# Low parts of the mixers' weights by an adding transfer instead of a subtraction on GpSimd or VectorE, with small steps moved off VectorE

## The chip, the cores and the metric

The kernel runs on one core of one Trainium2 chip. The metric is the device time of one execution in microseconds (us), median of three runs.

## The reference

One decoder layer over 512 tokens of width 1024, batch 1. `u = rmsnorm(x)` is projected by one wide matrix `w_in` into the inputs of two mixers. The first is a gated delta rule with 8 heads of 128 (q, k, v, an output gate z, a decay and a beta per head); the second is a sparse attention with 8 query heads and 2 key heads, for which an indexer scores keys and keeps the best 128 per query. Both results are gated and added, multiplied by `w_out`, and added to x. Then comes a ConvGLU feed-forward of width 2816, and a last RMS norm.

```
u     = rmsnorm(x, g1);  proj = u @ w_in
qkv   = silu(causal_dwconv(proj[:, 0:3072], w, width 4));  q, k = l2norm(q), l2norm(k)
o_gdn = rmsnorm(delta_rule(q, k, v, decay, beta)) * silu(z)
score[t,s] = sum_h iw[t,h] * relu(iq[t,h] . layernorm(ik)[s]);  keep the top 128 causal s
o_dsa = softmax(q k^T on the kept keys) v
h     = x + (sigmoid(ga) * o_gdn + sigmoid(gb) * o_dsa) @ w_out
out   = rmsnorm(h + (silu(conv(up_gate)) * conv(up_val)) @ w_down)
```

All arithmetic is float32 at the interface.

## The kernel before, in words

Every large product is made of three TensorE passes in the rounded type float32r. Both operands are split into a high part (`hi`, the value rounded to float32r) and a low part (`lo`, what is left over), and a product is `hi*lo + lo*hi + hi*hi`. The function `passes` (L202, L203, L204) issues the three matmuls. The weights lie in DRAM as pieces of 128 x 1024 floats (512 KB). `load` issues one piece's transfer on SyncE's queue into a buffer `raw`; `piece` then lets ScalarE copy `raw` to `whi` (L194, which rounds) and another engine, GpSimd or VectorE, subtract `raw - whi` into `wlo` (L195). There are three buffers of each. A chunk is two pieces. `channel_major` multiplies a chunk with all 512 tokens into two PSUM banks of 128 channels each (24 matmuls of 512 columns per piece); `token_major` makes tokens the rows (48 matmuls of 256 columns per piece). PSUM has three banks named `acc` for these.

In program order: the start loads the transposed x (`xT`), splits it (`xgh`, `xgl`) and computes the attention's values (`dv`) and a small projection (`sp`: indexer key, decay, beta, indexer weights) while pieces arrive. The factors 1/rms of the four token blocks (`r4`) are turned into a row by four diagonal matrices `dg` and a matmul with ones (`rp`), giving `rB`. Then `uTh`, `uTl` (the split normalized input) are made, and the indexer queries `iq` come from two chunks on the un-normalized `xg`, scaled afterwards by `rB` (`iqf`). `gdn_half(0)` and `gdn_half(1)` each do six chunks (k, q, v of four heads), a causal convolution with SiLU on VectorE and ScalarE (`conv_silu`), transposes with sums of squares (`sumsq`), a triangular inverse by forward substitution (`nn`, `wi`, `tw`: 60 dependent VectorE steps between two round trips through DRAM, `bl`), and a recurrence over four chunks (`TR`, `upd`, `kS`, `o`). VectorE also finds the top 128 scores (`top`, `mask`). The attention's 32 items (`lg`, `pe`, `pT`, `oB`) and the twelve gate chunks (z, ga, gb, `token_major`) follow. After them `w_out` (8 pieces) and the feed-forward (44 and 22 pieces) run with the same `piece`, with VectorE (for the first two chunks of the feed-forward GpSimd) as the engine of the low part. The mixers have 62 pieces that go through `piece`; the three pieces of the start are split by `split` (L231 to L234).

The order within each engine's queue is not the program's: the framework's scheduler lays the instructions out by a simulated timeline and then fixes one static order per engine. Every engine runs its queue in order, so an instruction that waits holds all behind it on its engine.

Of the kernel before, what the change touches and what calls it, by code (L numbers as in the profile page):

```python
# [86 lines left out]
def hybrid_block(ctx: ExitStack, tc: tile.TileContext, x: bass.AP, xc: bass.AP, wp: bass.AP,  # L87
# [90 lines left out]


    pipe = ctx.enter_context(tc.tile_pool(name="pipe", bufs=1))  # L180
    pipe.tile([128, 16], F, name="pad1")
    pos = [0]

    def load():
        raw = pipe.tile([128, 1024], F, name="raw", bufs=3)
        nc.sync.dma_start(raw, wp[pos[0]])
        pos[0] += 1
        hi = pipe.tile([128, 1024], R, name="whi", bufs=3)
        lo = pipe.tile([128, 1024], R, name="wlo", bufs=3)
        return raw, hi, lo  # L190

    def piece(lo_engine):
        raw, hi, lo = load()
        A.copy(hi, raw)  # L194
        lo_engine.tensor_sub(lo, raw, hi.bitcast(F))  # L195
        return hi, lo

    def passes(o, lhs, rhs, first, last, shared=False):
# [29 lines left out]
        for tb in tbs:  # L228
            nc.sync.dma_start(xt[tb], x[128 * tb:128 * tb + 128])

    def split(raw, hi, lo):  # L231
        for eng, c in ((V, slice(0, 512)), (P, slice(512, 1024))):
            A.copy(hi[:, c], raw[:, c])
            eng.tensor_sub(lo[:, c], raw[:, c], hi[:, c].bitcast(F))  # L234

    load_xT(0)
    nc.sync.dma_start(ch, chan)
    dvp = [load()]
    load_xT(1, 2, 3)
    dvp.append(load())  # L240
    load_xT(4, 5, 6, 7)
    sp = load()
    load_x(0, 1, 2, 3)
# [16 lines left out]

    for k in range(KT):
        x_part(k)
        if k % 4 == 0:
            split(*dvp[k // 4])
        dv_mm(k)
    split(*sp)
    for k in range(KT):
# [6 lines left out]
    rp = tp("rp")  # L274
    for tb in range(NT):
        dg = sl.tile([128, 128], F, name="dg", bufs=2)
        V.tensor_scalar(dg, ident, r4[:, tb:tb + 1], None, op0=OP.mult)
        T.matmul(rp[:, 128 * tb:128 * tb + 128], ones, dg, start=True, stop=True)
    V.tensor_copy(rB, rp)
    sr.release()  # L280
# [11 lines left out]
    def token_major(eng):  # L292

        pcs = [piece(eng), piece(eng)]
# [9 lines left out]
    def channel_major(eng, src=None, second=P):  # L304
        pcs = [piece(eng), piece(second)]
# [54 lines left out]
    A.copy(ikh, ikp)  # L360
    V.tensor_sub(ikl, ikp, ikh.bitcast(F))
    iw = const.tile([128, NT, 8], F, name="iw")
    V.tensor_scalar(iw, sm[:, :, 80:88], float((H ** -0.5) * (IDXD ** -0.5)), None, op0=OP.mult)


    def sc8(name):
# [48 lines left out]
    for k in range(KT):  # L415
# [2 lines left out]
        A.copy(uTh[:, k], uv)  # L418
        (V, P)[k % 2].tensor_sub(uTl[:, k], uv, uTh[:, k].bitcast(F))

    iq = []
    for j in range(2):
        for t, p in enumerate(channel_major(P, xg)):
            iqf = PR.tile([128, 512], F, name="iqf", tag="t", bufs=5)
            V.tensor_mul(iqf, p, rB)  # L425
            for s in range(2):
                q = PR.tile([128, 512], R, name="iq", tag="dqo", bufs=9)
                src = iqf[64 * s:64 * s + 64]
                A.copy(q[0:64], src)
                V.tensor_sub(q[64:128], src, q[0:64].bitcast(F))  # L430
                iq.append(q)
# [37 lines left out]
    def gdn_half(hh):  # L469
# [14 lines left out]
        def sumsq(src, dst, keep):  # L484
            for c in range(NT):
                p = rec("kqt")
                for h in range(HH):
                    T.transpose(p[:, 128 * h:128 * h + 128], src[:, h, 128 * c:128 * c + 128], ident)
                for h in range(HH):
                    A.activation(sqj, p[:, 128 * h:128 * h + 128], AF.Square, accum_out=dst[:, 0, c, h:h + 1])  # L490
                if keep is not None:
                    V.tensor_copy(keep[:, c], p.rearrange("p (h d) -> p h d", d=128))


        for j in range(2):
            for t, p in enumerate(channel_major(P, second=V if hh else P)):
# [4 lines left out]
        ks = sc("ks", 5)  # L501
        rk, mk, nk, bk, kd = (ks[:, i] for i in range(5))
# [4 lines left out]
        V.tensor_mul(kd, rk, kde[:, :, hs])  # L507

        for j in range(2):
            for t, p in enumerate(channel_major(P, second=V if hh else P)):  # L510
# [8 lines left out]
        for c in range(NT):  # L519
            ge = PL.tile([128, 2, HH, 128], F, name="ge", tag="g4", bufs=2)  # L520
            r0 = c * H + HH * hh
            A.dma_start(ge[:, 0], bass.AP(tensor=gdr.tensor, offset=gdr.offset + r0 * 128,
                                          ap=[[0, 128], [128, HH], [1, 128]]))
            P.affine_select(out=ge[:, 1], in_=ge[:, 0], pattern=[[0, HH], [1, 128]], base=0,
                            channel_multiplier=-1, compare_op=OP.is_ge, fill=NEG)
            for h in range(HH):
                A.activation(ge[:, 1, h], ge[:, 1, h], AF.Exp, bias=nG[:, c, HH * hh + h:HH * hh + h + 1])
            A.activation(ge[:, 0], ge[:, 0], AF.Exp)
            cs = slice(128 * c, 128 * c + 128)
            for h2 in range(2):  # L530
# [12 lines left out]
            for h in range(HH):  # L543
                A.activation(kt[:, c, h], kt[:, c, h], AF.Identity, scale=kd[:, c, h:h + 1])


        for j in range(2):
            for t, p in enumerate(channel_major(P, second=V if hh else P)):
# [79 lines left out]
        for c in range(NT):  # L628
# [62 lines left out]


    dk = PR.tile([128, 2, 512], F, name="dk", tag="k4", bufs=2)
    for t, p in enumerate(channel_major(P)):
        A.copy(dk[:, t], p)
    dq = []
    for j in range(4):
        for t, p in enumerate(channel_major(P)):
            q = half_kb("dq")
            A.copy(q, p)  # L700
            dq.append(q)
# [64 lines left out]
        V.scalar_tensor_tensor(o, t, 1.0, o, op0=OP.add, op1=OP.mult)  # L766

    def z_chunk(j):
        for t2, p in enumerate(token_major(P)):
# [5 lines left out]

    def ga_chunk(j):
        bias = gate_bias(256 * j)
        for t2, p in enumerate(token_major(P)):
            gated(oAv[j][:, 2 * t2:2 * t2 + 2], p, bias)

    def gb_chunk(j):
        bias = gate_bias(1024 + 256 * j)
        for t2, p in enumerate(token_major(P)):
            tb = slice(2 * t2, 2 * t2 + 2)
            t = tmp("tg")
            V.tensor_add(t, p, bias)
# [252 lines left out]
```

## Time and profile before

| | us |
|---|---|
| median of 3 runs | 965.05 (963.51 to 967.03) |
| the profiled execution's own time | 965.41 |
| its span in the trace | 963.4 |
| TensorE busy | 923.5 (96%) |
| VectorE, ScalarE, GpSimd busy | 615.2, 439.7, 205.3 |

The span is the time from the first to the last instruction of the program. Matmuls are pipelined and their ends are modelled, so a busy TensorE is one that has matmuls in flight. The granted clock of TensorE in a stretch is a share of its full speed: 1.00 is 2.4 GHz and 0.50 is 1.2 GHz.

### The profile page before, as it was taken

The page shows a single profiled execution, that of the slowest core. Times are in us where ns is not written, and L with a number is a line of the kernel's source. Part 1 is how long each engine was busy: PE and PEld are TensorE (multiplying, and loading weights), DVE is VectorE, ACT ScalarE, POOL GpSimd, SP SyncE. Part 2 cuts the span into 40 slices and gives each one's busy share as a digit, 9 for nine tenths or more (in the row PEclk, how much of TensorE's full clock was granted, in tenths as well). Part 3 has the DMA queues.
Part 4 walks back from the last instruction along what each step waited for, and adds up shares of the span by engine and source line. Part 5 has one row for each costly group of instructions (what it writes and reads, how often), then busy time and mean ns, then how long its engine had stood idle before and what let it go on. Part 6 is the DMA issues. An engine that isn't in the chain of part 4 may idle for free.

```text
span 963.4 us, 14652 instructions
## 1 busy us (share of the span) xinstructions
PE 923.5 (96%) x5671; PEld 806.4 (84%) x5671; DVE 615.2 (64%) x1262; ACT 439.7 (46%) x938; POOL 205.3 (21%) x120
## 2 busy tenths in 40 slices
PE   8889998989999898899999999999999999999997
PEld 8768887767787797899999999888888888888886
DVE  5997999897638948755543637556655666522424
ACT  7436673422458653345544436444444444421313
POOL 2744343520211254211154022100000000000201
PEclk9999999998999999999999999999999999999999
DMA  8222222324310122311322223323232332323212
GB/s 322 93 87 88 88 72 83 100 65 110 111 45 25 64 77 85 98 55 50 137 72 91 85 90 97 100 87 102 96 104 94 88 110 87 110 90 107 88 66 87
DMA packets 39541, 89.29 MB, mean 93 GB/s; under 512 B 15632, under 2 KB 16944, under 8 KB 39472
## 3 DMA queue, kind: packets, MB, share of 16 engines
q1 hardware_dynamic: 24048, 82.05, 26.0%
q10 hardware_dynamic: 15424, 6.31, 2.7%
q8 instruction: 44, 0.72, 0.3%
q14 instruction: 25, 0.20, 0.1%
HBM read 85.18 MB, written 3.16 MB: 92 GB/s over the span
## 4 chain that ended last, share of the span: by engine, by line
PE 66%; DVE 22%; DMA 5%; ACT 3%; issue 2%; POOL 1%; ACTq 0%; SPq 0%; DVEq 0%; POOLq 0%
PE acc L202 17%; PE acc L204 17%; PE acc L203 17%; PE d L202 3%; PE d L203 3%; PE d L204 3%; DVE y L460 3%; DVE wi L585 2%; DVE mask L689 2%; DVE tw L583 2%; DVE top L688 2%; PE lg L728 1%; PE lg L710 1%; DMA ge<-gdr 1%; DMA nn<-bl 1%
## 5 line engine op out<-in xcount | busy, mean ns | idle before, releaser
L194 ACT CAST whi<-raw 128x1024 fp32r<-128x1024 f32 x136 | 142.3, 1047 | 175.7 <-PE acc L204 77.0
L195 POOL TENSOR_TENSOR wlo<-raw,whi 128x1024 fp32r<-128x1024 f32 x60 | 147.5, 2460 | 295.4 <-ACT whi L194 248.2
L195 DVE TENSOR_TENSOR wlo<-raw,whi 128x1024 fp32r<-128x1024 f32 x76 | 94.3, 1241 | 147.5 <-ACT whi L194 147.4
L203 PE MATMUL acc<-hTh,wlo 128*128 128x512 f32 (+1 forms) x368 | 139.8, 380 | 0.0
L202 PE MATMUL acc<-hTl,whi 128*128 128x512 f32 (+1 forms) x368 | 139.1, 381 | 0.2 <-DVE hTl L837 0.2
L204 PE MATMUL acc<-hTh,whi 128*128 128x512 f32 (+1 forms) x368 | 138.8, 380 | 0.0
L202 PE MATMUL acc<-uTl,whi 128*128 128x512 f32 x272 | 109.1, 402 | 5.3 <-DVE iqf L425 4.3
L203 PE MATMUL acc<-uTh,wlo 128*128 128x512 f32 x272 | 108.9, 400 | 5.1 <-DVE wlo L195 5.1
L204 PE MATMUL acc<-whi,uTh 128*128 128x256 f32 x384 | 113.3, 295 | 0.0
L202 PE MATMUL acc<-wlo,uTh 128*128 128x256 f32 x384 | 112.2, 292 | 0.0
L203 PE MATMUL acc<-whi,uTl 128*128 128x256 f32 x384 | 112.1, 292 | 0.0
L204 PE MATMUL acc<-uTh,whi 128*128 128x512 f32 x272 | 108.9, 400 | 0.0
L979 POOL TENSOR_TENSOR h<-h,gf 128x512 f32<-128x512 f32 (+1 forms) x8 | 10.6, 1344 | 338.6 <-ACT sq L975 338.6
L896 DVE SCALAR_TENSOR_TENSOR fy<-acc,ch,fy 128x511 f32<-128x511 f32 x88 | 65.8, 748 | 26.2 <-ACT fy L894 24.7
L202 PEld LDWEIGHTS acc<-hTl,whi 128*128 128x128 f32 x368 | 69.2, 188 | 13.5 <-DVE hTl L837 0.4
L204 PEld LDWEIGHTS acc<-hTh,whi 128*128 128x128 f32 x368 | 69.2, 188 | 13.1
L203 PEld LDWEIGHTS acc<-hTh,wlo 128*128 128x128 f32 x368 | 69.2, 188 | 13.1
L202 PEld LDWEIGHTS acc<-wlo,uTh 128*128 128x128 f32 x384 | 73.9, 193 | 1.6 <-issue 1.0
L204 PEld LDWEIGHTS acc<-whi,uTh 128*128 128x128 f32 x384 | 73.8, 192 | 1.7 <-issue 1.0
L203 PEld LDWEIGHTS acc<-whi,uTl 128*128 128x128 f32 x384 | 74.0, 193 | 1.2 <-issue 1.0
L202 PEld LDWEIGHTS acc<-uTl,whi 128*128 128x128 f32 x272 | 52.1, 192 | 16.6 <-DVE iqf L425 4.8
L203 PEld LDWEIGHTS acc<-uTh,wlo 128*128 128x128 f32 x272 | 52.1, 191 | 15.5 <-DVE wlo L195 5.5
(313 smaller groups left out, 1916.9 us busy)
## 6 DMA issues: line engine op xcount, KB each, us to landing
raw<-in_wp_dram SPq DMA_DIRECT2D x139, 512.0 KB, 3.4
xT<-in_xc_dram SPq DMA_DIRECT2D x8, 256.0 KB, 6.0
xt<-in_x_dram SPq DMA_DIRECT2D x4, 512.0 KB, 7.8
ge<-gdr ACTq DMA_DIRECT2D x8, 256.0 KB, 3.4
h<-in_x_dram SPq DMA_DIRECT2D x4, 512.0 KB, 6.0
out_dram<-h SPq DMA_DIRECT2D x8, 256.0 KB, 2.2
gbias<-in_rows_dram ACTq DMA_DIRECT2D x8, 128.0 KB, 3.1
nn<-bl ACTq DMA_DIRECT2D x4, 256.0 KB, 4.8
```

What stands on the lines that cost most here:

```text
L194: A.copy(hi, raw)
L195: lo_engine.tensor_sub(lo, raw, hi.bitcast(F))
L202: a = T.matmul(o, lh, rl, start=first, stop=False, skip_group_check=shared)
L203: T.matmul(o, ll, rh, start=False, stop=False, skip_group_check=shared)
L204: return a, T.matmul(o, lh, rh, start=False, stop=last, skip_group_check=shared)
L460: V.scalar_tensor_tensor(y[:, s:], p[:, :512 - s], cw[:, ti, 3 - s:4 - s], y[:, s:], op0=OP.mult, op1=OP.add)
L583: V.tensor_mul(w, wi[:, 0:c, j:j + 1].to_broadcast([128, c, m]), nn[:, j:j + 1, j + 1:].to_broadcast([128, c, m]))
L585: V.tensor_sub(wi[:, 0:c, j + 1:], wi[:, 0:c, j + 1:], w)
L688: V.max(top, score[b])
L689: V.match_replace(score[b], top, score[b], TAKEN)
L896: V.scalar_tensor_tensor(y[:, s:], p[:, :512 - s], fw[:, ti, 2 - s:3 - s], y[:, s:], op0=OP.mult, op1=OP.add)
L979: P.tensor_mul(hv, hv, gf[:, 512 * half + c.start:512 * half + c.stop])
```

## The change

The low part of a mixer's piece is no longer a subtraction. ScalarE writes `-raw`, rounded to float32r, into `wlo`; this is `-hi`. Then a transfer issued by GpSimd reads the same piece from DRAM once more and adds it to `wlo` in SBUF, which leaves `raw - hi`. `whi` is copied by ScalarE as before. So each of the 62 pieces has a second ScalarE pass and a second transfer of 512 KB, and no subtraction. `raw` has two buffers instead of three for the whole kernel, `wlo` four instead of three. `w_out` and the feed-forward keep the subtraction.

Small steps go with it. The indexer's 1/rms is left out of the queries and multiplied into the indexer's weights `iw`. The key's l2 factor `rk` is left out of `at` and `kt` and put into the scale of `vt` (`mk` for `bk`), so `at` of two heads is one product. The copy of the transposed keys (`keep`) and the diagonals `dg` go from VectorE to ScalarE. The pieces of the start are loaded in halves, split in quarters by ScalarE and VectorE alone, and the constants `ch` are loaded on ScalarE's queue.

```diff
-    def load():
-        raw = pipe.tile([128, 1024], F, name="raw", bufs=3)
-        nc.sync.dma_start(raw, wp[pos[0]])
+    def load(parts=1):
+        raw = pipe.tile([128, 1024], F, name="raw", bufs=2)
+        n = 1024 // parts
+        for k in range(parts):
+            nc.sync.dma_start(raw[:, n * k:n * k + n], wp[pos[0]][:, n * k:n * k + n])
         pos[0] += 1
         hi = pipe.tile([128, 1024], R, name="whi", bufs=3)
-        lo = pipe.tile([128, 1024], R, name="wlo", bufs=3)
+        lo = pipe.tile([128, 1024], R, name="wlo", bufs=4)
         return raw, hi, lo

-    def piece(lo_engine):
+    def piece(lo_engine=None):
+        w = wp[pos[0]]
         raw, hi, lo = load()
-        A.copy(hi, raw)
-        lo_engine.tensor_sub(lo, raw, hi.bitcast(F))
+        if lo_engine is None:
+            A.activation(lo, raw, AF.Copy, scale=-1.0)
+            P.dma_start(lo, w, accum_op=OP.add)
+            A.copy(hi, raw)
+        else:
+            A.copy(hi, raw)
+            lo_engine.tensor_sub(lo, raw, hi.bitcast(F))
         return hi, lo
...
-    def split(raw, hi, lo):
-        for eng, c in ((V, slice(0, 512)), (P, slice(512, 1024))):
+    def split(raw, hi, lo, n=512, ks=None):
+        for k in range(1024 // n) if ks is None else ks:
+            c = slice(n * k, n * k + n)
             A.copy(hi[:, c], raw[:, c])
-            eng.tensor_sub(lo[:, c], raw[:, c], hi[:, c].bitcast(F))
+            V.tensor_sub(lo[:, c], raw[:, c], hi[:, c].bitcast(F))
+
+    A.dma_start(ch, chan)
     load_xT(0)
-    nc.sync.dma_start(ch, chan)
-    dvp = [load()]
+    dvp = [load(2)]
     load_xT(1, 2, 3)
-    dvp.append(load())
+    dvp.append(load(2))
...
-        if k % 4 == 0:
-            split(*dvp[k // 4])
+        split(*dvp[k // 4], n=256, ks=[k % 4])
...
-        V.tensor_scalar(dg, ident, r4[:, tb:tb + 1], None, op0=OP.mult)
+        A.activation(dg, ident, AF.Identity, scale=r4[:, tb:tb + 1])
...
-    V.tensor_scalar(iw, sm[:, :, 80:88], float((H ** -0.5) * (IDXD ** -0.5)), None, op0=OP.mult)
+    V.scalar_tensor_tensor(iw, sm[:, :, 80:88], float((H ** -0.5) * (IDXD ** -0.5)),
+                           r4.unsqueeze(2).to_broadcast([128, NT, 8]), op0=OP.mult, op1=OP.mult)
...
-            iqf = PR.tile([128, 512], F, name="iqf", tag="t", bufs=5)
-            V.tensor_mul(iqf, p, rB)
...
-                src = iqf[64 * s:64 * s + 64]
+                src = p[64 * s:64 * s + 64]
...
-                    V.tensor_copy(keep[:, c], p.rearrange("p (h d) -> p h d", d=128))
+                    A.copy(keep[:, c], p.rearrange("p (h d) -> p h d", d=128))
...
-                    V.scalar_tensor_tensor(at[:, c, h], p[:, i, 1], rk[:, c, h:h + 1], ge[:, 1, h],
-                                           op0=OP.mult, op1=OP.mult)
+                h = slice(2 * h2, 2 * h2 + 2)
+                V.tensor_mul(at[:, c, h], p[:, :, 1], ge[:, 1, h])
...
-                A.activation(kt[:, c, h], kt[:, c, h], AF.Identity, scale=kd[:, c, h:h + 1])
+                A.activation(kt[:, c, h], kt[:, c, h], AF.Identity, scale=kde[:, c, g:g + 1])
...
-                A.activation(vt[:, c, h], ps[:, h], AF.Identity, scale=bk[:, c, h:h + 1])
+                A.activation(vt[:, c, h], ps[:, h], AF.Identity, scale=mk[:, c, h:h + 1])
```

All calls of `channel_major` and `token_major` lose their engine argument, so all their pieces take the new branch; before, the second piece of each chunk in `gdn_half(1)` had its low part on VectorE.

The static orders change with it. On ScalarE, where the first two pieces of the indexer queries are split, stood before (`whi` are the high parts, `smT` is the small projection on its way to being transposed):

```order
L167 ACTIVATE rms<-ss_353,eps 128x1
L378 ACT_TABLE_LOAD
L378 ACTIVATE na<-rv 128x8
L756 DMA gbias<-in_rows_dram 128x256 x2
L194 CAST whi<-raw 128x1024 x2
L332 COPY smT<-acc 128x512
L194 CAST whi<-raw 128x1024
L375 ACTIVATE beta<-sm 128x32
```

and now stands:

```order
L389 ACT_TABLE_LOAD
L389 ACTIVATE na<-rv 128x8
L766 DMA gbias<-in_rows_dram 128x256
L200 ACTIVATE wlo<-raw 128x1024
L202 CAST whi<-raw 128x1024
L766 DMA gbias<-in_rows_dram 128x256
L200 ACTIVATE wlo<-raw 128x1024
L202 CAST whi<-raw 128x1024
L342 COPY smT<-acc 128x512
L287 ACTIVATE dg<-ident,r_177 128x128 x2
L200 ACTIVATE wlo<-raw 128x1024
```

Each piece has two rows, and the last two diagonals stand behind both pieces and `smT`.

On TensorE, just behind the small projection, stood before (`xgh`, `xgl` are the split input, `rp` the sums over the diagonals, `smp` the transposes of `smT`):

```order
L278 MATMUL rp<-dg,ones 128x128 x2
L202 MATMUL acc<-xgl,whi 128x512 x2
L278 MATMUL rp<-dg,ones 128x128
L335 MATMUL smp<-ident,smT 128x128 x4
L278 MATMUL rp<-dg,ones 128x128
L203 MATMUL acc<-xgh,wlo 128x512
L204 MATMUL acc<-xgh,whi 128x512
```

and now stands:

```order
L288 MATMUL rp<-dg,ones 128x128 x2
L212 MATMUL acc<-xgl,whi 128x512 x2
L213 MATMUL acc<-xgh,wlo 128x512
L214 MATMUL acc<-xgh,whi 128x512
L212 MATMUL acc<-xgl,whi 128x512
```

The first pass that reads a low part (`acc<-xgh,wlo`) now comes ahead of the transposes and of the other two diagonals, which moved 10 to 20 rows back.

On VectorE, in the forward substitution of the first half, stood before (`tw` is a product, `wi` the running inverse):

```order
L583 TENSOR_TENSOR tw<-wi,nn 128x126
L585 TENSOR_TENSOR wi<-wi,tw 128x9x14
L195 TENSOR_TENSOR wlo<-raw,whi 128x1024
L583 TENSOR_TENSOR tw<-wi,nn 128x117
L585 TENSOR_TENSOR wi<-wi,tw 128x9x13
```

and now stands:

```order
L593 TENSOR_TENSOR tw<-wi,nn 128x128
L595 TENSOR_TENSOR wi<-wi,tw 128x8x16
L593 TENSOR_TENSOR tw<-wi,nn 128x120
L595 TENSOR_TENSOR wi<-wi,tw 128x8x15
L593 TENSOR_TENSOR tw<-wi,nn 128x126
L595 TENSOR_TENSOR wi<-wi,tw 128x9x14
L593 TENSOR_TENSOR tw<-wi,nn 128x117
```

No low part of a weight stands on VectorE there any more.

## Rows read from the trace of the kernel before

**Rows 1.** The page, part 1: span, then busy us of each engine.
```profile
span 963.4 us, 14652 instructions
PE 923.5 (96%) x5671; PEld 806.4 (84%) x5671; DVE 615.2 (64%) x1262; ACT 439.7 (46%) x938; POOL 205.3 (21%) x120
```

**Rows 2.** Busy time by stretch: PE, PEld, DVE, ACT, POOL, clock, DMA share, GB/s.
```profile
20.00:66.00 46.00, 38.70 (x164) 31.18 (x163) 42.53 (x86) 22.12 (x33) 25.27 (x14) 0.93 0.30 99
66.00:140.00 74.00, 74.00 (x356) 61.61 (x355) 66.55 (x150) 48.97 (x138) 29.31 (x15) 1.00 0.27 86
140.00:200.00 60.00, 56.73 (x283) 46.42 (x282) 56.81 (x133) 25.32 (x58) 28.89 (x18) 1.00 0.33 100
200.00:300.00 100.00, 91.48 (x657) 75.81 (x657) 66.48 (x157) 42.78 (x105) 13.93 (x7) 0.97 0.24 69
300.00:420.00 120.00, 108.99 (x936) 99.71 (x935) 92.80 (x249) 63.59 (x194) 40.69 (x24) 0.99 0.25 71
420.00:580.00 160.00, 160.00 (x1336) 156.65 (x1335) 82.81 (x192) 74.28 (x178) 41.45 (x20) 1.00 0.27 90
...
620.00:963.40 343.40, 336.91 (x1548) 281.34 (x1546) 171.25 (x224) 124.90 (x169) 10.58 (x8) 1.00 0.29 95
```

**Rows 3.** The same view over the four stretches at half clock.
```profile
29.04:32.45 3.41, 3.09 (x8) 2.58 (x9) 3.12 (x9) 0.23 (x1) 2.51 (x2) 0.50 0.70 235
59.76:63.17 3.41, 3.41 (x10) 2.90 (x11) 3.21 (x9) 2.58 (x4) 1.08 (x1) 0.50 0.00 0
216.77:223.59 6.82, 6.07 (x14) 4.81 (x15) 6.10 (x23) 0.00 (x0) 0.00 (x0) 0.50 0.49 156
380.61:384.02 3.41, 3.41 (x17) 3.37 (x16) 3.27 (x5) 0.09 (x1) 2.12 (x1) 0.50 0.07 17
```

**Rows 4.** Waits of PE: us in total, times, longest.
```profile
PE pT L724 <- ACT pe L716: 5.6, 4, 2.4
PE acc L203 <- DVE wlo L195: 5.1, 1, 5.1
PE acc L202 <- DVE iqf L425: 4.3, 1, 4.3
PE kk L534 <- DVE at L540: 3.1, 5, 1.3
PE lg L710 <- ACT oB L732: 3.0, 5, 1.0
PE rp L278 <- DVE dg L277: 2.6, 2, 1.4
```

**Rows 5.** VectorE in order of time: start us, us, instruction.
```profile
25.20 4.10 DVE L277 TENSOR_SCALAR dg<-ident,r 128x128 f32<-128x128 f32 x2 [0.25 <-PE rp L278]
209.21 2.34 DVE L583 TENSOR_TENSOR tw<-wi,nn 128x105 f32<-128x105 f32 x1
216.25 1.22 DVE L195 TENSOR_TENSOR wlo<-raw,whi 128x1024 fp32r<-128x1024 f32 x1
```

**Rows 6.** Groups by line: busy us, mean ns | idle before, releaser.
```profile
L195 POOL TENSOR_TENSOR wlo<-raw,whi 128x1024 fp32r<-128x1024 f32 x60 | 147.5, 2460 | 295.4 <-ACT whi L194 248.2 <-DVE UT L595 22.3 <-issue 16.3
L194 ACT CAST whi<-raw 128x1024 fp32r<-128x1024 f32 x136 | 142.3, 1047 | 175.7 <-PE acc L204 77.0 <-PE d L204 70.3 <-issue 8.2
```

**Rows 7.** ScalarE, then TensorE, in order of time, around the first indexer piece.
```profile
23.43 1.98 ACT L194 CAST whi<-raw 128x1024 fp32r<-128x1024 f32 x2
27.39 0.60 PE L335 MATMUL smp<-ident,smT 128*128 128x128 f32 x4
29.80 0.77 PE L203 MATMUL acc<-xgh,wlo 128*128 128x512 f32 x1
```

**Rows 8.** DMA issues: KB each, median us to landing; then raw's range, 0 to 45.
```profile
raw<-in_wp_dram SPq DMA_DIRECT2D x139, 512.0 KB, 3.4
DMA to landing us min/median/max: 3.4/5.5/10.3
```

**Rows 9.** The line of the high parts from 66 to 140: ScalarE busy, count.
```profile
66.00:140.00 74.00, 11.43 (x11) 1.00 0.27 86
```

More of the change, by code (lines that the diff above doesn't have):

```diff
@@ L180, in hybrid_block @@
     pipe = ctx.enter_context(tc.tile_pool(name="pipe", bufs=1))
-    pipe.tile([128, 16], F, name="pad1")
+    pipe.tile([128, 48], F, name="pad1")
     pos = [0]
-    def load():
-        raw = pipe.tile([128, 1024], F, name="raw", bufs=3)
-        nc.sync.dma_start(raw, wp[pos[0]])
+    def load(parts=1):
[3 more added lines that the diff above has]
+            nc.sync.dma_start(raw[:, n * k:n * k + n], wp[pos[0]][:, n * k:n * k + n])
         pos[0] += 1
         hi = pipe.tile([128, 1024], R, name="whi", bufs=3)
-        lo = pipe.tile([128, 1024], R, name="wlo", bufs=3)
+        lo = pipe.tile([128, 1024], R, name="wlo", bufs=4)
         return raw, hi, lo
-    def piece(lo_engine):
+    def piece(lo_engine=None):
+        w = wp[pos[0]]
         raw, hi, lo = load()
-        A.copy(hi, raw)
-        lo_engine.tensor_sub(lo, raw, hi.bitcast(F))
+        if lo_engine is None:
[5 more added lines that the diff above has]
+            lo_engine.tensor_sub(lo, raw, hi.bitcast(F))
         return hi, lo
@@ L290, in u_blk, with token_major @@
         return uTh[:, k, 128 * tb:128 * tb + 128], uTl[:, k, 128 * tb:128 * tb + 128]
-    def token_major(eng):
-        pcs = [piece(eng), piece(eng)]
+    def token_major():
+        pcs = [piece(), piece()]
         ps = [acc().rearrange("p (t c) -> p t c", c=256) for _ in range(2)]
@@ L302, in token_major, with channel_major @@
         return ps
-    def channel_major(eng, src=None, second=P):
-        pcs = [piece(eng), piece(second)]
+    def channel_major(src=None):
+        pcs = [piece(), piece()]
         ps = [acc(), acc()]
@@ L422, in hybrid_block @@
     for j in range(2):
-        for t, p in enumerate(channel_major(P, xg)):
-            iqf = PR.tile([128, 512], F, name="iqf", tag="t", bufs=5)
-            V.tensor_mul(iqf, p, rB)
+        for p in channel_major(xg):
             for s in range(2):
                 q = PR.tile([128, 512], R, name="iq", tag="dqo", bufs=9)
-                src = iqf[64 * s:64 * s + 64]
+                src = p[64 * s:64 * s + 64]
                 A.copy(q[0:64], src)
@@ L491, in sumsq @@
                 if keep is not None:
-                    V.tensor_copy(keep[:, c], p.rearrange("p (h d) -> p h d", d=128))
+                    A.copy(keep[:, c], p.rearrange("p (h d) -> p h d", d=128))
         for j in range(2):
-            for t, p in enumerate(channel_major(P, second=V if hh else P)):
+            for t, p in enumerate(channel_major()):
                 conv_silu(p, 8 + HH * hh + 2 * j + t, kT[:, 2 * j + t])
@@ L500, in gdn_half @@
         rk0 = rsqrt_of(ssk.rearrange("p o t h -> p (o t h)"), 16, "rk").rearrange("p (t h) -> p t h", h=HH)
-        ks = sc("ks", 5)
-        rk, mk, nk, bk, kd = (ks[:, i] for i in range(5))
+        ks = sc("ks", 4)
+        rk, mk, nk, bk = (ks[:, i] for i in range(4))
         V.tensor_copy(rk, rk0)
@@ L506, in gdn_half @@
         V.tensor_mul(nk, rk, ssk[:, 0])
-        V.tensor_mul(kd, rk, kde[:, :, hs])
         for j in range(2):
-            for t, p in enumerate(channel_major(P, second=V if hh else P)):
+            for t, p in enumerate(channel_major()):
                 conv_silu(p, HH * hh + 2 * j + t, qT[:, 2 * j + t])
@@ L539, in gdn_half @@
                                            op0=OP.mult, op1=OP.mult)
-                    V.scalar_tensor_tensor(at[:, c, h], p[:, i, 1], rk[:, c, h:h + 1], ge[:, 1, h],
-                                           op0=OP.mult, op1=OP.mult)
+                h = slice(2 * h2, 2 * h2 + 2)
+                V.tensor_mul(at[:, c, h], p[:, :, 1], ge[:, 1, h])
             P.tensor_mul(qT[:, :, cs], qT[:, :, cs], ge[:, 0])
             for h in range(HH):
-                A.activation(kt[:, c, h], kt[:, c, h], AF.Identity, scale=kd[:, c, h:h + 1])
+                g = HH * hh + h
+                A.activation(kt[:, c, h], kt[:, c, h], AF.Identity, scale=kde[:, c, g:g + 1])
         for j in range(2):
-            for t, p in enumerate(channel_major(P, second=V if hh else P)):
+            for t, p in enumerate(channel_major()):
                 h = 2 * j + t
@@ L693, in hybrid_block @@
     dk = PR.tile([128, 2, 512], F, name="dk", tag="k4", bufs=2)
-    for t, p in enumerate(channel_major(P)):
+    for t, p in enumerate(channel_major()):
         A.copy(dk[:, t], p)
@@ L697, in hybrid_block @@
     for j in range(4):
-        for t, p in enumerate(channel_major(P)):
+        for t, p in enumerate(channel_major()):
             q = half_kb("dq")
@@ L768, in z_chunk @@
     def z_chunk(j):
-        for t2, p in enumerate(token_major(P)):
+        for t2, p in enumerate(token_major()):
             t = tmp("tz")
@@ L777, in ga_chunk @@
         bias = gate_bias(256 * j)
-        for t2, p in enumerate(token_major(P)):
+        for t2, p in enumerate(token_major()):
             gated(oAv[j][:, 2 * t2:2 * t2 + 2], p, bias)
@@ L782, in gb_chunk @@
         bias = gate_bias(1024 + 256 * j)
-        for t2, p in enumerate(token_major(P)):
+        for t2, p in enumerate(token_major()):
             tb = slice(2 * t2, 2 * t2 + 2)
```

## The prediction

> **What bounds the kernel now.** I read the page's first part, then the busy time by stretch with the granted clock, then the waits of TensorE, then the timeline of VectorE and ScalarE around the longest waits. The page shows TensorE with matmuls in flight for 923.5 of 963.4 us [rows 1], and the change removes none of its matmuls, so what can be won is idle time and slow clock. By stretch [rows 2] TensorE is idle for 7.3 us from 20 to 66 us (46.00 less 38.70), not at all to 140, 3.3 to 200, 8.5 to 300, 11.0 to 420, not at all to 580; from 620 on it is busy but for 6.5 us, all in a part that the change touches only by a buffer. So 30.1 us of idle time lie where the mixers run. Besides, TensorE was granted 0.50 (1.2 GHz) in four stretches, 17.05 us together (3.41, 3.41, 6.82 and 3.41) [rows 3], each behind an idle time of TensorE; at 2.4 GHz the same matmuls take half, so 8.5 us more are lost. The most that a better order of the other engines can give is 30.1 + 8.5 = 38.6 us.
>
> Who is waited for [rows 4]: VectorE for a low part (5.1 us, once), for `iqf` (4.3, once), for `at` (3.1), for the diagonals (2.6); ScalarE for `pe` and `oB` (8.6). Why VectorE is late is in its timeline. Two diagonals took 4.10 us, while GpSimd subtracted; and a product of 105 columns took 2.34 us, while the subtraction beside it, with 1024 columns, needs 1.22 [rows 5]. So VectorE stands still for whole subtractions of GpSimd, which take 2.46 us each, 60 times [rows 6].
>
> **The change part by part.** The sum is made against the profiled execution's own time, 965.4 us, which lies 0.4 above the median of the runs.
>
> *The low part that VectorE made.* At 212 us TensorE waits 5.1 us for a subtraction that stands in VectorE's queue behind the forward substitution and starts at 216.25 [rows 5]; the wait is followed by 6.82 us at half clock [rows 3], which cost 3.4. In the new order no subtraction stands there. Its replacement hangs on ScalarE and a transfer, and both are free: ScalarE is busy 43% from 200 to 300 and the DMA engines 24% [rows 2]. I take both away: -8.5. Bounds: -8.5, and 0 if the new low part is as late.
>
> *The indexer's factor.* `iqf` goes, and with it the dependence of the PSUM banks on `rB`, which came late behind the two diagonals. The bank is now held for two copies and two subtractions instead of one product, but three banks serve four tiles. I take away the wait of 4.3 and half of the 3.41 us behind it at half clock: -6.0. Bounds: -6.0 and 0.
>
> *The diagonals, and the first low part.* The wait of 2.6 us goes, but the new order has TensorE read the first low part ahead of the transposes and the other diagonals. When does it come? ScalarE began the high parts at 23.43 [rows 7]; two small diagonals now stand ahead in its queue, so I let `-raw` run from 23.7 to 24.7. Then comes the adding transfer. No row shows one issued by GpSimd, nor one that adds. The nearest is the plain load of the same bytes: 3.4 us to landing as a rule, 3.4 to 10.3 with median 5.5 where the queues are full, as in the first 45 us [rows 8]. I take 5.5: landing at 30.2, against 29.80 for that matmul before [rows 7], and 0.60 us of transposes [rows 7] and about 0.5 of sums, done by then before, are still to do. So +1.5; bounds -0.6 (3.4) and +6.3 (10.3). Below nothing it can't go much further, since ScalarE's copy is where it was.
>
> The Trainium skill's page "DMA: Bandwidth & Descriptors" (section "Anatomy of one DMA — SWDGE (gpsimd) path") gives a transfer issued by GpSimd 2.0 us and the bytes at 436 GB/s, an estimate of 3.2 us here; by it this term would be -0.8 and the sum -18.8. The page "Collectives: The Full Stack" (section "The bandwidth ceiling: the fold count and why AG ≠ RS ≠ AR") says that an add in a DMA costs a second read and halves the rate; no row here shows it.
>
> *VectorE's small steps.* Without GpSimd's subtractions its products run at their own length, `at` is one operation per two heads, and the copies of the keys are gone. Of the 3.1 us of waits for `at` I take half, -1.5; bounds 0 and -3.1.
>
> *The waits for ScalarE.* 5.6 + 3.0 us and half of the last 3.41 at half clock, 10.3 together, are chains of VectorE and ScalarE in the attention. VectorE gets faster, ScalarE gets more to do: 62 copies of 1047 ns are 65 us, and the key copies and diagonals some 6. From 20 to 580 us ScalarE is busy for 277 us (the sum of six rows of rows 2); 348 of 560 is 62%, so it is no bound on average, but each copy can hold a chain by its length. I take -2; bounds -10.3 and +25 (one piece per 9 us, as 62 pieces in 560 us are, gives 24 copies in the 220 us from 200 to 420, each 1.05 us, all on the path).
>
> *What costs nothing, and its cover.* The adding transfers in steady state: ScalarE's order writes a `wlo` about three pieces ahead of TensorE, and a piece's 24 matmuls take some 5.7 us (60 pieces in the last 343.4 us), so 5.5 us hide under 15. If the transfers take longer than that, each piece waits. The DMA engines: a piece's load keeps all 16 busy 0.29 x 5.7 = 1.7 us; an add that costs as much again or twice that makes 3.4 to 5.0 per piece, of 6.7 us that a piece has from 66 to 140 (11 pieces in 74 us) [rows 9]. GpSimd: 60 subtractions leave, 62 issues come. Two `raw` buffers in the feed-forward: copy 1.05 [rows 6], subtraction 1.22 [rows 5], load 3.4 make 5.7 us of the 11.4 that two pieces give; if ScalarE or VectorE come 5 us late, it costs that. The start in halves: the second row of x lands no earlier, so 0, bounds -1.6 and +1.
>
> The sum: -8.5 - 6.0 + 1.5 - 1.5 - 2 = -16.5, so 949 us.
>
> **The rivals.** *ScalarE takes VectorE's place.* In-order, it holds `pe`, `oB` and the transposed keys behind copies that wait for loads. For: the two ScalarE waits of rows 4 are already the largest together, and ScalarE is 53% busy from 300 to 420. Against: 66 to 140 has it 66% busy with TensorE never idle. With the upper bound of that term the sum is -14.5 + 25, some 975 us; it is slower than before once more than 14 of these 24 copies stand on the path.
>
> *The adding transfer is slow.* For: nothing shows one. Against: 5 us of engine time per piece would still fit. Beyond that, at 7 us a piece needs 8.7 of DMA and has 6.7 from 66 to 200: 20 pieces times 2.0 are +40, less the gains, 989 us. It decides from 5.0 us of engine time, three times the plain load's. A late descriptor would do the same: that VectorE's long operations keep GpSimd from issuing, at 1.2 us apiece (the longest of rows 5 that is not itself held) against a lead of 15, would cost nothing, and only queues of them would. Beside it stands the Trainium skill's page "SBUF — State Buffer" (section "Who interferes with whom"): GpSimd can't write descriptors while VectorE runs certain copies and scalar operations, which speaks against issuing on GpSimd; no row shows it yet.
>
> *The waits only move.* VectorE's relief is taken by the next chain (the DRAM round trips of `bl`, the recurrence), and only the low part's wait goes, with the indexer's clock: -5 us, 960. For: the order is static and chains run through four engines. Against: in two of the waits the late instruction itself leaves.
>
> *All of it goes.* TensorE then runs through: 965.4 - 38.6 + 1.5 = 928. Against: four of the waits are not touched by any edit.
>
> **How the numbers follow.** The forecast, 940 to 958 us, has 0.56; the waits move (958 to 967), 0.15; nearly all goes (under 940), 0.11; ScalarE, 0.10; the slow transfer, 0.08. About 0.3% (2.9 us) is what a measurement of this kernel can tell. Below 962.2 lie the forecast, the larger gain and half of the moved waits: 0.75. Within 0.3%: the rest of the moved waits, 0.08. Slower: 0.17. The range, 928 to 972, takes in the larger gain and part of ScalarE's case, and leaves out the slow transfer.
>
> **What would show it.** Right: TensorE's wait for `wlo` at 212 and for `iqf` at 55 gone with their half-clock stretches; VectorE's small operations at their own length; the adding transfers landing within 6 us; TensorE idle 20 to 30 us in all. Wrong: a wait of TensorE for `wlo` in more than one place, or DMA share near 1 in the stretches to 200 (slow transfer); waits for `pe`, `oB`, `sqj` or `y` that add up to over 20 us (ScalarE); a feed-forward longer than 343 us (the `raw` buffers).

## The result, and the profile after

The changed kernel takes 979.28 us (median of 4 runs, 976.81 to 984.97) against 964.83 for the kernel before beside it: ratio 1.016, 95% interval 1.014 to 1.0181. It is slower; the prediction was 949 us. The profiled execution took 976.81 us.

The page's first and third part: busy time by engine, then the DMA queues with packets, MB and their share of 16 engines' span (q0 is the queue that GpSimd issues on).

```profile
span 975.1 us, 14737 instructions
PE 926.2 (95%) x5671; PEld 808.4 (83%) x5671; DVE 547.7 (56%) x1229; ACT 497.4 (51%) x1016; POOL 116.7 (12%) x123
...
q1 hardware_dynamic: 24192, 81.91, 24.2%
q0 software_dynamic: 8928, 32.51, 19.9%
```

VectorE lost 67.5 us of busy time and GpSimd 88.6 against [rows 1]. But 62 adding transfers used 19.9% of 16 engines for 975.1 us: 0.199 x 975.1 / 62 = 3.13 us of all 16 engines each.

The same stretches as [rows 2]: PE, PEld, DVE, ACT, POOL, clock, DMA share, GB/s.

```profile
20.00:66.00 46.00, 37.26 (x166) 30.15 (x165) 29.29 (x81) 27.07 (x42) 13.47 (x13) 0.93 0.69 164
66.00:140.00 74.00, 71.07 (x328) 57.66 (x327) 52.72 (x133) 58.74 (x155) 11.38 (x15) 0.98 0.72 163
140.00:200.00 60.00, 57.02 (x283) 47.65 (x283) 54.15 (x158) 32.92 (x62) 14.46 (x17) 0.97 0.68 157
200.00:300.00 100.00, 90.71 (x626) 74.95 (x625) 46.42 (x116) 49.10 (x96) 11.64 (x14) 0.95 0.61 141
300.00:420.00 120.00, 105.07 (x774) 96.59 (x772) 74.70 (x237) 79.07 (x229) 22.50 (x24) 0.99 0.52 115
420.00:580.00 160.00, 159.21 (x1456) 154.66 (x1457) 77.03 (x191) 82.94 (x184) 17.62 (x18) 0.99 0.51 129
```

The DMA engines went from 0.24 to 0.33 up to 0.51 to 0.72. TensorE is idle for 38.9 us up to 420, against 30.1 before. The waits of TensorE (us in total, times, longest), which answer to [rows 4]:

```profile
PE m L611 <- DVE UT L605: 10.1, 2, 5.4
PE acc L213 <- DMA wlo<-in_wp_dram: 6.2, 1, 6.2
PE lg L720 <- ACT oB L742: 5.9, 6, 1.4
PE vt L563 <- DVE at L550: 2.7, 1, 2.7
PE pT L734 <- ACT pe L726: 2.6, 2, 1.9
PE rel L453 <- DVE mask L460: 2.5, 2, 1.8
PE acc L212 <- DVE iq L440: 2.3, 1, 2.3
```

The waits for VectorE's low part and for `iqf` are gone (2.3 us of the latter are left as `iq`, the copies from the bank). In their place stand the end of the triangular inverse (`UT`) and the first adding transfer. Half clock went from 17.05 us in four stretches [rows 3] to 30.72 in six, of which three (same columns):

```profile
28.42:35.25 6.83, 3.28 (x8) 2.60 (x9) 0.00 (x0) 1.99 (x2) 0.86 (x1) 0.50 1.06 253
...
229.81:236.64 6.83, 5.61 (x57) 4.22 (x59) 6.16 (x9) 4.72 (x6) 1.72 (x2) 0.50 0.74 116
...
417.54:424.37 6.83, 4.05 (x18) 3.81 (x19) 3.79 (x7) 1.28 (x4) 0.45 (x1) 0.50 0.95 201
```

The DMA issues (KB each, median us to landing; [rows 8] has raw at 3.4; the last row is the kernel before):

```profile
raw<-in_wp_dram SPq DMA_DIRECT2D x137, 512.0 KB, 3.7
wlo<-in_wp_dram POOLq DMA_DIRECT2D x62, 512.0 KB, 6.9
...
bl<-wi ACTq DMA_DIRECT2D x4, 128.0 KB, 7.0
...
bl<-wi ACTq DMA_DIRECT2D x4, 128.0 KB, 2.9
```

Why `UT` is late is in the chain of waits from 212 to 236 us (start us, us, what):

```profile
214.35 0.19 DVE wi L595
...
214.58 0.50 DVE UT L603
215.07 0.49 ACTq L597
...
215.60 12.40 DMA bl<-wi
...
228.07 2.18 DMA MT<-bl
...
230.28 0.71 DVE UT L605
...
231.03 0.31 PE m L611 x2
```

VectorE finished the forward substitution at 214.5 and stored from 215; before, that store was issued at 224.6, so VectorE had become almost 10 us earlier. The round trip through DRAM gave most of it back: the first product that reads `UT` begins at 231.03, against 233.0 before, and TensorE waits 5.4 us for it. 128 KB needed 12.40 us. In the kernel before, the same leg was

```profile
225.16 4.82 DMA bl<-wi
```

Two adding transfers had been issued at 215.11 and 216.54 and a load of `raw` at 217.69, and while they ran the DMA engines were full (the columns of [rows 2]; the share is 1.02):

```profile
220.00:225.00 5.00, 5.00 (x23) 4.13 (x22) 0.00 (x0) 0.00 (x0) 0.00 (x0) 1.00 1.02 228
```

And because the last leg, `MT<-bl`, is issued from ScalarE's queue, ScalarE stood for 10.6 us behind it (ScalarE in order of time; in brackets the idle time before):

```profile
218.46 1.05 ACT L202 CAST whi<-raw 128x1024 fp32r<-128x1024 f32 x1 [0.80 <-PE acc L214]
228.07 1.94 ACTq L599 DMA_DIRECT2D MT<-bl  x4
230.11 1.06 ACT L200 ACTIVATE wlo<-raw 128x1024 fp32r<-128x1024 f32 x1 [10.60 <-issue]
```

ScalarE's longest class of waits is new altogether (in the kernel before, it waited for loads at the start alone, 2.6 us):

```profile
ACT wlo L200 <- DMA raw<-in_wp_dram: 78.4, 27, 6.2
```

From the first matmul of the feed-forward to the last it is 363.4 us in both kernels, so the whole loss lies in the mixers.

### The profile page after: what moved, and what is told of

Same layout as the page of the kernel before. It is cut to its first block, busy times and chain, and to the rows that moved or that the text cites. A ratio compares the mean times of both kernels' runs of the same rounds, so it can differ in the third digit from the quotient of the medians.

```text
span 975.1 us, 14737 instructions
## 1 busy us (share of the span) xinstructions
PE 926.2 (95%) x5671; PEld 808.4 (83%) x5671; DVE 547.7 (56%) x1229; ACT 497.4 (51%) x1016; POOL 116.7 (12%) x123
## 3 DMA queue, kind: packets, MB, share of 16 engines
q0 software_dynamic: 8928, 32.51, 19.9%
## 4 chain that ended last, share of the span: by engine, by line
PE 59%; DMA 18%; DVE 10%; ACT 10%; issue 2%; POOL 0%; ACTq 0%; SPq 0%; DVEq 0%; POOLq 0%
PE acc L214 15%; PE acc L213 15%; PE acc L212 15%; DMA raw<-in_wp_dram 11%; PE d L212 3%; PE d L213 3%; PE d L214 3%; ACT wlo L200 2%; ACT whi L202 2%; DMA ge<-gdr 2%; DMA nn<-bl 1%; DMA bl<-wi 1%; DVE mask L699 1%; PE lg L720 1%; PE lg L738 1%
## 5 line engine op out<-in xcount | busy, mean ns | idle before, releaser
L205 DVE TENSOR_TENSOR wlo<-raw,whi 128x1024 fp32r<-128x1024 f32 x70 | 87.0, 1244 | 140.4 <-ACT whi L204 140.3
L200 ACT ACTIVATE wlo<-raw 128x1024 fp32r<-128x1024 f32 x62 | 65.6, 1058 | 100.7 <-DMA raw<-in_wp_dram 78.4
L201 POOL DMA_DIRECT2D wlo<-in_wp_dram x62 | 53.9, 869 | 364.4 <-ACT wlo L200 296.9
L470 DVE SCALAR_TENSOR_TENSOR y<-acc,cw,y 128x511 f32<-128x511 f32 (+2 forms) x72 | 52.7, 742 | 23.1 <-ACT y L468 22.3
```

The source lines that it names most:

```text
L200: A.activation(lo, raw, AF.Copy, scale=-1.0)
L201: P.dma_start(lo, w, accum_op=OP.add)
L470: V.scalar_tensor_tensor(y[:, s:], p[:, :512 - s], cw[:, ti, 3 - s:4 - s], y[:, s:], op0=OP.mult, op1=OP.add)
```

## The experiments

The first four: what is the loss? One theory is that the adding transfers fill the DMA engines; the rivals are the two `raw` buffers, the 62 added passes of ScalarE, and the small edits. Only the kernels with a plain transfer (here and at the end) keep the change's static order word for word; in the others the order is laid out anew, and their differences hold an effect of the order that was not measured apart.

**No transfer.** The low part stays `-hi`; ScalarE's passes and the buffers stay.

```diff
-            P.dma_start(lo, w, accum_op=OP.add)
+            del w
```

> The changed kernel without the adding transfer: the low part of the mixers' weights stays -hi, both ScalarE passes and the two raw buffers remain. Theory 1 (the transfers fill the DMA engines, 3.1 us of all 16 per piece, and so lengthen every load and every round trip through DRAM on the chains): 948 to 962 us; ScalarE's waits for raw fall from 78 us to under 25, a bl<-wi transfer lands in about 3 us as before the change (7.0 now), TensorE's 10 us of waits for the inverse (m <- UT) go. Theory 2 (two raw buffers: a load can only be issued when ScalarE has read the one two pieces back, and ScalarE's queue then stands before it): 970 us or more, ScalarE still waits over 60 us for raw. Theory 3 (62 more passes on ScalarE are the price): 970 us or more, with waits of TensorE for ScalarE over 15 us.

922.72 us (922.18 to 923.19), ratio 0.9565 (0.955 to 0.958), far below what any theory gave. TensorE is idle for some 2 us from 20 to 580 us and at half clock nowhere there:

```profile
span 921.5 us, 14596 instructions
...
PE 910.9 (99%) x5671; PEld 800.4 (87%) x5671; DVE 543.3 (59%) x1229; ACT 498.6 (54%) x1016; POOL 62.1 (7%) x61
```

So ScalarE's 62 passes cost nothing (its busy time is the same as in the change), two `raw` buffers cost nothing by themselves, and what the change frees is worth 42 us (with the order laid out anew). The transfer costs 56.6.

**Plain transfer.** The same bytes, issued at the same place, overwrite instead of adding.

```diff
-            P.dma_start(lo, w, accum_op=OP.add)
+            P.dma_start(lo, w)
```

> The changed kernel with a plain transfer of the same bytes from GpSimd in place of the adding one (the low part is then the weight itself); every engine's order is the same, row for row. Theory 1: the transfer's share of the DMA engines falls from 3.1 to about 1.7 us per piece, raw and the round trips land 1 to 3 us earlier, 966 to 973 us. Theories 2 and 3: 976 to 982 us, no change.

940.46 us (938.21 to 949.43), ratio 0.9767 (0.9717 to 0.9816), again below every theory: of the 56.6 us the add alone makes 38.8, at the same order. By the two intervals this is good to some 5 us. Queue q0 and the landing of the transfer on its page, then TensorE's wait for `UT`:

```profile
q0 software_dynamic: 8928, 32.51, 12.1%
...
wlo<-in_wp_dram POOLq DMA_DIRECT2D x62, 512.0 KB, 3.9
```
```profile
PE m L611 <- DVE UT L605: 2.3, 1, 2.3
```

A plain transfer takes 0.121 x 936.5 / 62 = 1.83 us of all engines against 3.13, and lands in 3.9 us against 6.9. Since each matmul of the one trace has its twin in the other, the lag of the change can be read off matmul by matmul (start in the change less start here, us):

```
at start (change)   85   168   231   272   287   337   357   399   420   end
lag                2.9   8.4  17.2  21.2  23.0  27.3  30.4  32.7  36.1  38.6
```

It comes in more than a dozen steps: 5.5 at the first `UT`, 2.8 at `vt` behind `at`, 2.4 at the second `UT`, 2.1 at the first transfer, 1 to 2 each at `rel`, `upd`, `pT`, `kqt`, `lg`, and what the half clock takes behind them. These are two executions, and single steps hold the chance of one (see the last experiment).

**Three raw and three wlo buffers**, the adding transfer kept.

```diff
-        raw = pipe.tile([128, 1024], F, name="raw", bufs=2)
+        raw = pipe.tile([128, 1024], F, name="raw", bufs=3)
...
-        lo = pipe.tile([128, 1024], R, name="wlo", bufs=4)
+        lo = pipe.tile([128, 1024], R, name="wlo", bufs=3)
```

> The changed kernel with three buffers of raw and three of the low part instead of two and four. Theory 2: ScalarE's waits for raw fall from 78 us to under 20, 958 to 968 us. Theory 1: the DMA engines stay as full and bl<-wi as slow, waits for low parts come in, 972 to 985 us. Theory 3: about 979 us.

961.72 us (958.67 to 963.15), ratio 0.997 (0.9955 to 0.9986): 17.6 us of the loss go. ScalarE no longer waits for loads; the longest waits of its low-part pass, and those of TensorE, are now

```profile
ACT wlo L200 <- PE acc L213: 35.2, 20, 9.5
```
```profile
PE acc L213 <- DMA wlo<-in_wp_dram: 12.3, 5, 6.3
PE m L611 <- DVE UT L605: 10.9, 2, 6.6
```

So two buffers of `raw` do cost, but only beside the adding transfers (without them TensorE was hardly idle with two). How much of the 17.6 us is the buffers and how much the new order was not measured. The round trip's wait stays.

**The small edits alone.** Subtractions as before (GpSimd, VectorE in the second half's second pieces), three and three buffers.

```diff
-    def channel_major(src=None):
-        pcs = [piece(), piece()]
+    def channel_major(src=None, second=P):
+        pcs = [piece(P), piece(second)]
```

> The small edits alone (indexer factor, key factor, key copies, diagonals, the start in halves and quarters), the low parts subtracted on GpSimd and VectorE as before the change, three raw and three low buffers. Theories 1 to 3, by which the transfers and what goes with them cost all: 950 to 962 us, since VectorE has less to do. Theory 4 (the small edits load ScalarE at the wrong places): 966 us or more.

965.67 us, ratio 1.0028 (1.0009 to 1.0047). They neither win nor lose anything worth the name. Two of TensorE's waits there show part of the reason: the low part is late as before, and the wait for `iqf` has become one for the copies from the bank.

```profile
PE acc L213 <- DVE wlo L205: 5.1, 1, 5.1
PE acc L212 <- DVE iq L440: 4.1, 1, 4.1
```

**The transfer alone**: the kernel before with the new branch of `piece` and two and four buffers, none of the small edits.

```diff
-        pcs = [piece(eng), piece(second)]
+        pcs = [piece(None), piece(None)]
```

> The kernel before with the adding transfer alone (two raw buffers and four wlo, as in the change), none of the small edits. If the transfer is the whole loss and the small edits are worth about nothing, as they were alone (ratio 1.003): 975 to 983 us. If the small edits win where the transfers leave VectorE free, and the transfers hide it: 985 us or more. If the small edits do harm beside the transfers (ScalarE fuller by diagonals and key copies): under 972 us.

978.28 us (976.94 to 980.03), ratio 1.0138 (1.0123 to 1.0153): the loss comes with the transfer and its buffers, and the small edits have no part in it that could be told.

The next five ask what, then, the 42 us are that came free, and what in the add is dear.

**All low parts on VectorE**, no transfer, with the small edits and three and three buffers (`token_major` alike):

```diff
-    def channel_major(src=None):
-        pcs = [piece(), piece()]
+    def channel_major(src=None, second=V):
+        pcs = [piece(V), piece(second)]
```

> Small edits, three raw and three wlo buffers, no adding transfer; all 62 low parts are subtracted on VectorE instead of 60 of them mostly on GpSimd. If what the transfer freed was VectorE from standing still for GpSimd's subtractions (2.43 us each against 1.24 on VectorE), 945 to 958 us, with VectorE at its own length in the short steps. If it freed VectorE from work as such, VectorE is now the bound: 968 us or more, with waits of TensorE for wlo, y and UT on VectorE.

942.17 us (941.11 to 943.64), ratio 0.9764 (0.9749 to 0.9778): even below the range of the first theory, though all 62 subtractions are now VectorE's.

**The kernel before, all low parts on VectorE**, at every such call, and nothing else:

```diff
-            for t, p in enumerate(channel_major(P, second=V if hh else P)):
+            for t, p in enumerate(channel_major(V, second=V)):
...
-        for t2, p in enumerate(token_major(P)):
+        for t2, p in enumerate(token_major(V)):
```

> The kernel before with one edit: all 62 low parts of the mixers are subtracted on VectorE, none on GpSimd, and nothing of the change. If GpSimd's subtractions were what held the kernel before, and the small edits are worth about nothing: 940 to 950 us. If the small edits make the room on VectorE that the subtractions need (with them it was 942): 953 us or more.

943.36 us (942.57 to 945.19), ratio 0.979 (0.977 to 0.981). VectorE got more work and the kernel got faster. Of this kernel first the page, with the busy times and VectorE's subtractions (busy us, mean ns), then VectorE's short products (min/median/max ns):

```profile
PE 919.9 (98%) x5671; PEld 808.1 (86%) x5671; DVE 619.4 (66%) x1318; ACT 440.5 (47%) x938; POOL 71.9 (8%) x64
...
L195 DVE TENSOR_TENSOR wlo<-raw,whi 128x1024 fp32r<-128x1024 f32 x132 | 164.4, 1246 | 157.7 <-ACT whi L194 157.7
```
```profile
L583 DVE TENSOR_TENSOR tw<-wi,nn x60: 162/251/303, 165.9 to 396.7; 128x110 f32<-128x110 f32 x6, 128x120 f32<-128x120 f32 x6, 128x30 f32<-128x30 f32 x4, 128x56 f32<-128x56 f32 x4
```

and the two rows that answer to them in the kernel before:

```profile
L195 DVE TENSOR_TENSOR wlo<-raw,whi 128x1024 fp32r<-128x1024 f32 x76 | 94.3, 1241 | 147.5 <-ACT whi L194 147.4
```
```profile
L583 DVE TENSOR_TENSOR tw<-wi,nn x60: 181/256/2336, 192.5 to 395.6; 128x110 f32<-128x110 f32 x6, 128x120 f32<-128x120 f32 x6, 128x30 f32<-128x30 f32 x4, 128x56 f32<-128x56 f32 x4
```

56 more subtractions are 164.4 - 94.3 = 70.1 us of work, but VectorE's busy time rose by 619.4 - 615.2 = 4.2 only. So some 66 us of the 615.2 in [rows 1] were VectorE standing behind GpSimd, counted as busy; the product of up to 2336 ns is at most 303 now. In the kernel before, each of the eight steps of `tw` and `wi` that took over 0.5 us ran beside a subtraction or a product (`at<-at,tz`) of GpSimd; the one such step that is left here, a `wi` of 1276 ns, runs beside that product. The Trainium skill's page "SBUF — State Buffer" (section "Who interferes with whom") says that a VectorE instruction with two SBUF inputs contends with a GpSimd instruction that reads SBUF, and the later one waits whole; these rows agree.

**Half of the transfers**: as with three and three buffers, the first piece of each chunk adding, the second on VectorE.

```diff
-        pcs = [piece(), piece()]
+        pcs = [piece(), piece(V)]
```

> As e3 (three raw and three wlo buffers, small edits), but only the first piece of each chunk has the adding transfer and the second is subtracted on VectorE: 31 transfers. If the loss is queueing on the DMA engines, it falls by more than half as their share falls from 0.7 to about 0.5: 940 to 953 us, with the round trip's wait (UT) under 5 us. If each transfer costs the same, it lies between the kernels with all and with none: 960 to 966 us. If VectorE's 31 subtractions hold its chains: over 966 us.

944.45 us (941.39 to 946.55), ratio 0.9784 (0.9762 to 0.9806). With half the transfers the loss against this kernel without transfers (942) is all but gone, so it is not proportional to their number. TensorE's wait for `UT` is down to 3.6 us.

**The add reads SBUF**: as with three and three buffers, the transfer takes the piece from `raw`.

```diff
-            P.dma_start(lo, w, accum_op=OP.add)
+            P.dma_start(lo, raw, accum_op=OP.add)
```

> As e3, but the adding transfer reads the piece from raw in SBUF instead of from DRAM; the same sum. If the add is what the 16 engines spend the time on: still about 3.1 us of all 16 per transfer, landing near 7, and 955 to 968 us. If the second read of DRAM is the cost: 1.7 to 2.0 us per transfer and 940 to 950 us, as with the plain transfer. raw is held until the transfer has landed, which with three buffers may add waits of ScalarE for raw: up to 975 us by that alone.

945.23 us (944.51 to 947.06), ratio 0.9792 (0.9776 to 0.9808). Queue q0, and the landing:

```profile
q0 software_dynamic: 8928, 32.51, 18.8%
...
wlo<-raw POOLq DMA_DIRECT2D x62, 512.0 KB, 5.1
```

0.188 x 945.2 / 62 = 2.87 us per transfer: the add, not the read of DRAM, keeps the engines busy. But it lands 2.1 us earlier than with three buffers and DRAM (7.2), and the kernel is 16.5 us faster; neither theory had both. How much of that is the landing and how much the new order stays open.

**Half of the transfers, from SBUF**: the last two together.

> Small edits, three raw and three wlo buffers; the first piece of each chunk has an adding transfer that reads raw in SBUF, the second is subtracted on VectorE. If what is left of the loss with half the transfers is still the DMA engines, it gets faster than the 944.5 us of the half that reads DRAM: 930 to 940 us. If what is left is a chain of VectorE and ScalarE: 942 to 948 us.

937.21 us (936.22 to 938.1), ratio 0.972 (0.9698 to 0.9742): faster than both kernels, and the fastest that leaves nothing out. Compared with the half that reads DRAM it is 7.2 us less, which speaks for the transfers as part of what was left there; the new order may have a share.

**Three plain transfers in the change.** Is it the filling as a whole, or single collisions? The two transfers beside the first round trip of `wi` and the one beside the second overwrite instead of adding; 59 add, and every engine's order is that of the change.

```diff
-            P.dma_start(lo, w, accum_op=OP.add)
+            P.dma_start(lo, w, **({} if pos[0] - 4 in (28, 29, 48) else {"accum_op": OP.add}))
```

> The change with only 3 of its 62 adding transfers plain (they overwrite instead of adding): the two issued beside the first half's round trip of wi through DRAM and the one beside the second half's; the order of every engine is the same. If the loss sits where an adding transfer stands beside a transfer that a chain waits for: the waits of TensorE for UT fall from 10.1 to under 6 us with the half-clock stretch behind them, bl<-wi lands 3 to 6 us earlier, and the time falls by 5 to 14 us, to 965 to 974. If the whole filling of the DMA engines is the cause and no single transfer: 3/62 of the 39 us between plain and adding, 2 us, 975 to 979.

972.62 us (971.33 to 976.89), ratio 1.0098 (1.0069 to 1.0127): by the medians 6.7 us less than the change with 3 of 62 transfers altered, where a share by number would be 1.9. The chain's leg of 12.40 us, and TensorE's waits for `UT` (10.1 us in the change; 6.6 is a little more than was expected), have become

```profile
213.31 7.90 DMA bl<-wi
```
```profile
PE m L611 <- DVE UT L605: 6.6, 3, 2.5
```

But the lag of the change behind this kernel, matmul by matmul (us), says less than the medians:

```
at start (change)   160   172   214   237   300   415   424   440   end
lag                 0.0   3.9   3.9   8.8   6.6   6.4  10.9   5.7   4.1
```

The first altered transfer is issued at 215 in the change, so the 3.9 us at 214 arose where the two kernels have the same instructions: that is the chance of one execution. Behind it the first round trip gains 4.9 us, the half clock after it included, and the second 4.5; later waits take this back, and 0.2 of it is left at the end. So an adding transfer beside a transfer that a chain waits for does hold that chain up by some 5 us. How much of the time these three cost, and whether it is more than their share by number, the runs leave open. The 38.8 us as a whole are shown by the plain transfer; how they divide among the loads and the chains is not.

## Why the prediction was wrong

**The step that failed** is "What costs nothing, and its cover". It set the adding transfer against the lead of the weights ("5.5 us hide under 15") and the engines' time against a piece's time ("3.4 to 5.0 per piece, of 6.7 us"). Both covers held: landing took 6.9 us, still under 15, and 1.7 + 3.1 = 4.8 of 6.7 is the 0.72 of the row from 66 to 140. TensorE waited for the transfers' `wlo` once only, at the start. But with a share of 0.7 on average, and 1.02 beside the round trip, other transfers through the same engines came late: `bl<-wi` went from 2.9 to 7.0 us in the median (4.1 without the transfers and 6.1 with plain ones, so the median alone is not the add) and 12.40 at worst (no transfer of `bl` took over 6.0 and 7.4 us there), `raw` was waited for 27 times, and ScalarE, which issues or waits for both, passed it on. The prediction priced no other user of the DMA engines. The price of the transfer was 56.6 us, not the 1.5 of the sum. None of the signs that it named for being wrong came up: one place with a wait for `wlo`, a share of 0.72 at most in the rows from 20 to 200 us, 9.7 us of waits for `pe`, `oB`, `sqj` and `y` together.

**Two `raw` buffers** were weighed for the feed-forward, where they cost nothing (363.4 us in both). In the mixers, where each piece now has to stay in `raw` for two passes of an in-order ScalarE and its load comes late, they cost up to 17.6 us, the new order included.

**The slow-transfer rival** had the right side and nearly the size (989 us; measured 979), but its point of decision was wrong: it was to decide from 5.0 us of engine time, and 3.13 were enough, because it too asked for throughput alone. That its 989 lies near is luck: it is 20 pieces held up by 2.0 us each, and TensorE waited for one. *The waits only move* named the right place, the round trips of `bl`, but at their old length, and so gave 960. The page "Collectives: The Full Stack" of the Trainium skill (section "The bandwidth ceiling: the fold count and why AG ≠ RS ≠ AR") has an add halve the rate; the runs say 1.83 against 3.13 us, 0.58 of the rate. It stood in the prediction and was not carried through to the other users of the engines. The descriptors were no trouble here: all 62 issues of GpSimd took 0.856 to 1.023 us.

**The gains** were under-sized, not over-sized. Without the transfer all 42 us come, more than the 38.6 that were called the most and not the 18 that the terms gave. VectorE's stalls behind GpSimd were read from two rows [rows 5] and then priced at the few waits that end on VectorE directly (-8.5, -6.0, -1.5). The later waits, for `pe`, `oB` and `sqj`, were in the main its delay handed on: with no transfer and all of ScalarE's passes they are 0.7 (`oB`) and 0.2 us (`pe`). So "ScalarE takes VectorE's place" falls, and "All of it goes" was right as to what the relief can do.

**Term by term** in the change: the low part's wait at 212 went, as predicted, and came back as the round trip's, 5.4 us at 225 with 6.83 us at half clock, so -8.5 became about nothing. `iqf`: 4.3 us and 3.41 at half clock became 2.3 and none, -3.7 of the -6.0. The first low part: landing was estimated at 5.5, the matmul came at 31.97 instead of 30.2 and the wait of 6.2 brought 6.83 us at half clock; with the 2.6 of the diagonals and the 3.41 gone that is 6.2 - 2.6 + 3.4 - 1.7 = +5.3, within the bound of +6.3 but not +1.5. `at`: 2.7 instead of 3.1, not -1.5. The waits for ScalarE: 8.5 (`oB`, `pe`) for 8.6, not -2. Together these terms make about +1 us; the profiled execution was 11.4 longer. The rest lies in the main in waits for which the sum had no term: the second half's `UT` (4.6 us, with 6.83 at half clock behind it), `rel` (2.5), `upd` and `kqt` (1.4 each).

## What to carry to other kernels

A transfer that is hidden for its own reader is not free: list who else goes through the DMA engines (round trips, loads into few buffers, issues on a busy engine's queue) and price their delay, not only the throughput (here the mean share from 20 to 580 us was 0.59 with all transfers, 56.6 us slower than none, and 0.44 with half of them, 2 us slower than VectorE alone). Before work is moved off a slow engine, look at what that engine does to its neighbour: a short instruction with a maximum many times its median says it, and here one word (subtract on VectorE, not GpSimd) was worth 2.1%, where the small edits were worth next to nothing. A trace with the same order and one property changed lets the loss be read off instruction by instruction, once the stretch ahead of the first difference has shown how far two executions lie apart by chance.

## What the runs showed of the hardware

- By the times of its packets, an adding transfer of 512 KB kept all 16 engines 3.13 us (DRAM to SBUF) or 2.87 (SBUF to SBUF), a plain one 1.83; they landed after 6.9, 5.1 and 3.9 us in the median. GpSimd needed 0.87 us to issue the adding one and 0.55 the plain one:

```profile
L201 POOL DMA_DIRECT2D wlo<-in_wp_dram x62 | 53.9, 869 | 364.4 <-ACT wlo L200 296.9
```
```profile
L201 POOL DMA_DIRECT2D wlo<-in_wp_dram x62 | 33.8, 546 | 342.4 <-ACT wlo L200 292.0
```

- VectorE's busy time held some 66 us of standing still behind GpSimd in the kernel before; it shows in no wait.
- With the DMA engines at 0.6 to 0.7 of their time on average, a 128 KB transfer with a median of 2.9 us in the kernel before took 7.0, and 12.40 where they were full.
